# One shape for every product: 256 moving columns, and all moving operands 448 bytes past the stationary blocks modulo 512

## The chip, the cores and the metric

The kernel runs on one core of one Trainium2 chip. The metric is the device time of one execution in microseconds (us), the median of three runs. The core's engines are TensorE (PE in the rows, with its weight loads on a row of their own, PEld), VectorE (DVE), ScalarE (ACT), GpSimd (POOL) and SyncE (SP), which issues the transfers. A product on TensorE has a stationary operand (128 x 128, put in place by a weight load) and a moving operand, whose columns are streamed through it; the result is added up in PSUM.

## The reference

Two layers work on 256 tokens of 2048 features, all in float32. Each layer is a mixer and a gated feed-forward network, each added to the running state `h`.

```python
def reference(x, ...):
    h = x
    for i in range(DEPTH):              # DEPTH = 2
        j = i // 2
        if i % 2 == 0:
            h = h + conv_pool_mixer(h, ...)    # layer 0
        else:
            h = h + short_conv_mixer(h, ...)   # layer 1
        h = h + swiglu(rms_norm(h, ffn_norm[i]), w_gate[i], w_up[i], w_down[i])
    return rms_norm(h, final_norm)

def swiglu(h, w_gate, w_up, w_down):
    return (jax.nn.silu(h @ w_gate) * (h @ w_up)) @ w_down
```

`conv_pool_mixer` multiplies by `w_in` (2048 x 3072), runs a causal convolution of width 31 and four pooling windows, multiplies by small pooling matrices, and then by `w_out` (2048 x 2048). `short_conv_mixer` multiplies by `w_in` (2048 x 6144), runs a convolution of width 3 and two gates, and multiplies by `w_out`. `D_FF` is 5632.

## The kernel before

Activations are held with features on the 128 partitions and the 256 tokens along the row. All weights together are 5904 blocks of 128 x 128; they stand in one long array in the order in which they are used, and SP fetches them 16 blocks at a time. For float32 accuracy each block is split in two parts: `hi`, a rounded copy made by ACT (L124), and `lo`, the rest, made by DVE or, in part of the first stage, POOL (L131). Eight blocks are split at a time; six such pieces are held. The activations are split in the same way, so that a row of a moving operand holds 256 columns of high parts and then 256 columns of low parts (`xs`, `cat`, `y`, `z`). A block's contribution is hi x high + hi x low + lo x high.

`product` issues these on PE in one of two forms:

- **Wide** (L173, L174): one matmul with `hi` stationary and all 512 moving columns, which puts hi x high in the left half of an accumulator and hi x low in its right half, and one with `lo` and 256 columns, added to the right half. Two weight loads, 768 columns. Both feed-forward networks and layer 1's mixer use it: 5226 blocks. What is done with the result then begins with an addition of the two halves: ACT copies the right half to a tile `cross` (L198 in `summed`, L332 in `project`) and DVE adds it (L200, L333).
- **Narrow** (L176, L177, L178): three matmuls of 256 columns into one sum: `hi` on the high part, `hi` on the low part (with `hi` loaded again) and `lo` on the high part. Three weight loads, 768 columns. Layer 0's mixer uses it (656 blocks), and the very last output chunk (22 blocks, by `narrow_end`).

An accumulator `acc` has a PSUM bank of its own in either form; there are five.

The order of the work is that of the code, changed by a scheduler that places instructions by a time model; PE goes through the blocks in the order of the weight array. `matmul_chunks` takes blocks from `next_block`, which keeps the split four pieces ahead of PE. In layer 0's mixer `tick` hands out the steps of the convolution to DVE, ACT and POOL between the products.

The stages, with the names in the rows: layer 0's mixer (0 to 256 us; moving operand `xs`, then `cat`), the first feed-forward network (`xs` and `y`), layer 1's mixer (`xs` and `z`), the second feed-forward network (`xs` and `y`), the final norm.

Where a moving operand begins is set by a constant for each stage: `XS_M0`, `XS_F0` and so on are bytes from the start of a room that is somewhat larger than the operand (`moving`). Every `hi` and `lo` tile of the built program begins 64 bytes past a multiple of 512 in its partition's row, and a block takes 512 bytes, so each stationary block begins there too. A chunk of a moving operand takes 2048 bytes, 1024 for each half. So each stage has one distance between a moving operand's start and a stationary block's start modulo 512. By the addresses in the built program it is:

| moving operand | form | blocks | bytes past the stationary block, modulo 512 |
|---|---|---|---|
| `xs`, layer 0's mixer | narrow | 512 | 288 |
| `cat`, layer 0's mixer | narrow | 144 | 32 |
| `xs`, the later stages | wide | 3584 | 416 |
| `y` and `z` | wide | 1642 | 160 |
| `y`, last chunk | narrow | 22 | 160 |

Of the kernel before, what the change touches and what calls it, by code (L numbers as in the profile page):

```python
# [11 lines left out]
F32 = mybir.dt.float32  # L12
# [5 lines left out]
P = 128  # L18
# [56 lines left out]
KEEP = 8  # L75


XS_M0 = 32
XS_F0 = 160
XS_M1 = 160  # L80
XS_F1 = 160
Y_F0 = 64
Y_F1 = 64
Z_M1 = 64
CAT = 0

POOL_SPLIT = range(96, 24 * NC + 16 + 7 * NC + 8)

# [6 lines left out]
def block_kernel(ctx: ExitStack, tc: tile.TileContext, xT: bass.AP, xtok: bass.AP, vec: bass.AP, wall: bass.AP, out: bass.AP):  # L95
# [72 lines left out]
                if q:  # L168
                    q.popleft()[1]()

    def product(acc, hi, lo, x, first, last, wide):
        if wide:
            nc.tensor.matmul(acc, hi, x, start=first, stop=False, skip_group_check=True)  # L173
            nc.tensor.matmul(acc[:, T:], lo, x[:, :T], start=False, stop=last, skip_group_check=True)  # L174
        else:
            nc.tensor.matmul(acc[:, :T], hi, x[:, :T], start=first, stop=False)  # L176
            nc.tensor.matmul(acc[:, :T], hi, x[:, T:], start=False, stop=False)  # L177
            nc.tensor.matmul(acc[:, :T], lo, x[:, :T], start=False, stop=last)  # L178

    def matmul_chunks(xs, ks, n=1, wide=False, behind=None):  # L180


        accs = [ps.tile([P, 2 * T], F32, name="acc") for _ in range(n)]
        for i, k in enumerate(ks):
            first, last = i == 0, i == len(ks) - 1
            for acc in accs:
                hi, lo = next_block()
                product(acc, hi, lo, xs[:, k, :], first, last, wide)
                tick()
            if behind is not None:  # L190
                behind(k)
        return accs

    phase = [None]

    def summed(acc, name):
        t = phase[0].tile([P, T], F32, name="cross", bufs=3)
        nc.scalar.copy(t, acc[:, T:])  # L198
        s = (phase[0] if name == "pv" else tmp).tile([P, T], F32, name=name, bufs=2)
        nc.vector.tensor_tensor(out=s, in0=acc[:, :T], in1=t, op=ALU.add)  # L200
        return s

    def split(dst, src, scale=None):

# [10 lines left out]
    def col(name, i):  # L215
        return v[:, VECS[name] + i : VECS[name] + i + 1]
# [5 lines left out]
    def moving(room, at, n):  # L222

        return room[:, at // 4 : at // 4 + n * 2 * T].rearrange("p (c t) -> p c t", c=n)
# [96 lines left out]
            nc.vector.tensor_copy(out=r, in_=st)  # L321
            return r

    def project(src, ks, norm=None, wide=False, narrow_end=False):

        for n in range(NC):
            if narrow_end and n == NC - 1:
                wide = False
            (acc,) = matmul_chunks(src, ks, wide=wide)
            if wide:  # L330
                t = phase[0].tile([P, T], F32, name="cross", bufs=3)
                nc.scalar.copy(t, acc[:, T:])  # L332
                nc.vector.tensor_tensor(out=h[:, n, :], in0=h[:, n, :], in1=t, op=ALU.add)  # L333
            nc.vector.tensor_tensor(out=h[:, n, :], in0=acc[:, :T], in1=h[:, n, :], op=ALU.add)  # L334
            if norm is not None:
                norm.add(n)

    def scaled(acc, r, name, wide=False):
        if not wide:
            s = (phase[0] if name == "pv" else tmp).tile([P, T], F32, name=name, bufs=2)  # L340
            nc.vector.tensor_tensor(out=s, in0=acc[:, :T], in1=r, op=ALU.mult)
            return s
        s = summed(acc, name)
        nc.vector.tensor_tensor(out=s, in0=s, in1=r, op=ALU.mult)
        return s


    norm = Norm("mix_norm_e", XS_M0)
    xs = norm.xs
    nc.sync.dma_start(v[:, :NC], vec[:, :NC])  # L350

# [32 lines left out]
    with tc.tile_pool(name="m0", bufs=1) as m0, tc.tile_pool(name="ps_side", bufs=2, space=PSUM) as ps_side:  # L384
# [1 line left out]
        a_in = m0.tile([P, NA, pad + T], F32, name="a_in")  # L386
        nc.gpsimd.memset(a_in[:, :, :pad], 0.0)
        conv = m0.tile([P, NA, T], F32, name="conv")
        cat = moving(m0.tile([P, NA * 2 * T + 32], F32R, name="cat"), CAT, NA)
        total = m0.tile([P, 2, T], F32, name="total")  # L390

        sides, prods, state = {}, {}, {}
# [104 lines left out]
        def gated(acc_v, acc_g, c):  # L497
            gate = scaled(acc_g, r, "gate")
            nc.scalar.activation(gate, gate, AF.Sigmoid)
            val = acc_v[:, :T]  # L500
            nc.vector.tensor_tensor(out=val, in0=val, in1=r, op=ALU.mult)
            nc.vector.tensor_tensor(out=a_in[:, c, pad:], in0=val, in1=gate, op=ALU.mult)
            if c % 2:
                convolve(c - 1)
# [9 lines left out]
        def pooled(g):  # L514


            w = WINDOWS[g]
            xp = m0.tile([P, 2, pp + T], F32, name="xp", bufs=2)
            nc.gpsimd.memset(xp[:, :, :pp], 0.0)
            less = m0.tile([P, 2, T], F32, name="pm", bufs=2)  # L520
            for j in range(2):
                (acc,) = matmul_chunks(xs, every)
                nc.vector.tensor_tensor(out=xp[:, j, pp:], in0=acc[:, :T], in1=r, op=ALU.mult)
                nc.scalar.activation(less[:, j, :], xp[:, j, pp:], AF.Copy, scale=-float(w))
            cur, step = xp, 1
            while step < w:
                nxt = m0.tile([P, 2, pp + T], F32, name="sw", bufs=2)
                lo = pp - (w - 2 * step)
                nc.gpsimd.tensor_tensor(out=nxt[:, :, lo:], in0=cur[:, :, lo:], in1=cur[:, :, lo - step : pp + T - step], op=ALU.add)
                cur, step = nxt, 2 * step  # L530
            nc.gpsimd.tensor_tensor(out=cur[:, :, pp : pp + w - 1], in0=cur[:, :, pp : pp + w - 1], in1=corr[:, g, :, : w - 1], op=ALU.mult)
            nc.gpsimd.tensor_tensor(out=less, in0=cur[:, :, pp:], in1=less, op=ALU.add)
            dst = cat[:, 2 * g : 2 * g + 2, :]
            nc.scalar.activation(dst[:, :, :T], less, AF.Copy, scale=1.0 / w)
            nc.vector.scalar_tensor_tensor(out=dst[:, :, T:], in0=less, scalar=1.0 / w, in1=dst[:, :, :T], op0=ALU.mult, op1=ALU.subtract)
            relief.append(1)
# [8 lines left out]
        for g in POOL_ORDER:  # L545
            for j in range(2):
                (acc,) = matmul_chunks(cat, range(2 * g, 2 * g + 2))
                split(xs[:, 2 * g + j, :], acc[:, :T], col("pool_scale", 2 * g + j))

        project(xs, POOL_CHUNKS)  # L550
        drain()
        norm = Norm("ffn_norm0", XS_F0)
        project(cat, range(NA), norm)

    def swiglu(norm, following, at):
        with tc.tile_pool(name="ffn", bufs=1) as fp:
            phase[0] = fp
            y = moving(fp.tile([P, NH * 2 * T + 32], F32R, name="y"), at, NH)
            r = None
            for half in range(2):  # L560
                for f in range(NH):
                    (acc_g,) = matmul_chunks(norm.xs, every, wide=True)
                    (acc_u,) = matmul_chunks(norm.xs, every, wide=True)
                    if r is None:
                        r = norm.rstd()
                    gate = scaled(acc_g, r, "gate", True)
                    up = scaled(acc_u, r, "val", True)
# [3 lines left out]
                project(y, range(NH), following if half else None, wide=True, narrow_end=half and following.final)  # L571

    x0.close()


    after = Norm("mix_norm_o", XS_M1)
    swiglu(norm, after, Y_F0)


    norm = Norm("ffn_norm1", XS_F1)  # L580
    with tc.tile_pool(name="m1", bufs=1) as m1:
        phase[0] = m1
        z = moving(m1.tile([P, NC * 2 * T + 32], F32R, name="z"), Z_M1, NC)
        pad = SW - 1
        r = None
        for c in range(NC):
            (acc_c,) = matmul_chunks(after.xs, every, wide=True)
            (acc_v,) = matmul_chunks(after.xs, every, wide=True)
            if r is None:
                r = after.rstd()  # L590
            cg = scaled(acc_c, r, "gate", True)
            vv = scaled(acc_v, r, "val", True)
# [8 lines left out]
            (acc_b,) = matmul_chunks(after.xs, every, wide=True)  # L601
            bg = scaled(acc_b, r, "pv", True)
            nc.vector.tensor_tensor(out=bg, in0=bg, in1=co, op=ALU.mult)
            split(z[:, c, :], bg)
        project(z, every, norm, wide=True)


    last = Norm("final_norm", final=True)
    swiglu(norm, last, Y_F1)
# [93 lines left out]
```

## Time and profile before

| | |
|---|---|
| runs | 2094.73 us median, 2094.72 to 2096.01 us (3 runs) |
| span of the profiled execution, first to last instruction | 2093.2 us |
| granted clock of TensorE over the span | 0.996 |
| weight transfers | 365 of 1024 KB, 4.8 us from issue to landing |
| HBM traffic over the span | 188 GB/s |

The profiled execution has no time of its own beside its span; the median of the runs is 1.5 us above that span, which is what lies before the first and after the last instruction. The page of the profile gives busy time by engine, then the chain of waits that ended last, then groups of instructions. The busy time of a matmul contains its way through the array, and one matmul begins before the one before it has ended; how long PE takes for a matmul is therefore read from one start to the next and not from the duration in the row.

### The profile page before, as it was taken

The page shows a single profiled execution, that of the slowest core. Times are in us where ns is not written, and L with a number is a line of the kernel's source. Part 1 is how long each engine was busy: PE and PEld are TensorE (multiplying, and loading weights), DVE is VectorE, ACT ScalarE, POOL GpSimd, SP SyncE. Part 2 cuts the span into 40 slices and gives each one's busy share as a digit, 9 for nine tenths or more (in the row PEclk, how much of TensorE's full clock was granted, in tenths as well). Part 3 has the DMA queues.
Part 4 walks back from the last instruction along what each step waited for, and adds up shares of the span by engine and source line. Part 5 has one row for each costly group of instructions (what it writes and reads, how often), then busy time and mean ns, then how long its engine had stood idle before and what let it go on. Part 6 is the DMA issues. An engine that isn't in the chain of part 4 may idle for free.

```text
span 2093.2 us, 31608 instructions
## 1 busy us (share of the span) xinstructions
PE 2070.2 (99%) x12584; PEld 1850.5 (88%) x12584; DVE 1383.1 (66%) x1979; ACT 1061.8 (51%) x1571; POOL 200.5 (10%) x180
## 2 busy tenths in 40 slices
PE   8998999999999999999999999999999999999998
PEld 8998988888888888888888888888888888888887
DVE  6998766666556666666777777766666556666654
ACT  7886654444444444455444445554444444444453
POOL 2995200000000000011000001100000000000011
PEclk9999999999999999999999999999999999999999
DMA  8555455555555455555555555455555555555551
GB/s 322 190 199 181 151 190 184 193 189 186 196 184 198 182 195 188 188 195 183 189 191 184 198 182 199 181 186 197 182 195 187 190 193 184 199 183 195 187 191 71
DMA packets 56884, 395.53 MB, mean 189 GB/s; under 512 B 6432, under 2 KB 7200, under 8 KB 9760
## 3 DMA queue, kind: packets, MB, share of 16 engines
q1 hardware_dynamic: 56736, 393.52, 51.9%
q8 instruction: 98, 1.61, 0.3%
q14 instruction: 50, 0.41, 0.1%
HBM read 391.39 MB, written 2.10 MB: 188 GB/s over the span
## 4 chain that ended last, share of the span: by engine, by line
PE 98%; DMA 1%; DVE 1%; ACT 0%; SPq 0%; issue 0%; DVEq 0%; ACTq 0%
PE acc L173 57%; PE acc L174 29%; PE acc L176 4%; PE acc L178 4%; PE acc L177 3%; DMA rows<-in_xtok 0%; DMA h<-in_xT 0%; DVE res L620 0%; ACT hi L124 0%; PE st L252 0%; DVE lo L131 0%; PE st L283 0%; SPq L114 0%; ACT conv L492 0%; PE idle L258 0%
## 5 line engine op out<-in xcount | busy, mean ns | idle before, releaser
L131 DVE TENSOR_TENSOR lo<-w,hi 128x1024 fp32r<-128x1024 f32 (+1 forms) x691 | 846.2, 1225 | 634.3 <-ACT hi L124 630.1
L124 ACT CAST hi<-w 128x1024 fp32r<-128x1024 f32 (+1 forms) x740 | 775.5, 1049 | 963.9 <-PE acc L173 615.9
L173 PE MATMUL acc<-xs,hi 128*128 128x512 f32 x3584 | 1243.2, 392 | 0.0
L174 PE MATMUL acc<-xs,lo 128*128 128x256 f32 x3584 | 1002.3, 280 | 0.0
L173 PEld LDWEIGHTS acc<-xs,hi 128*128 128x128 f32 x3584 | 672.7, 188 | 148.5
L174 PEld LDWEIGHTS acc<-xs,lo 128*128 128x128 f32 x3584 | 672.7, 188 | 0.1
L173 PE MATMUL acc<-y,hi 128*128 128x512 f32 x1386 | 480.4, 392 | 0.0
L174 PE MATMUL acc<-y,lo 128*128 128x256 f32 x1386 | 386.8, 280 | 0.0
L173 PEld LDWEIGHTS acc<-y,hi 128*128 128x128 f32 x1386 | 259.9, 188 | 57.2
L174 PEld LDWEIGHTS acc<-y,lo 128*128 128x128 f32 x1386 | 260.2, 188 | 0.4
L314 POOL TENSOR_TENSOR sumsq<-sumsq,sq 128x256 f32<-128x256 f32 x56 | 59.0, 1053 | 1593.0 <-ACT sq L312 1593.0
L176 PE MATMUL acc<-xs,hi 128*128 128x256 f32 x512 | 142.7, 282 | 5.2 <-ACT hi L124 4.2
L177 PE MATMUL acc<-xs,hi 128*128 128x256 f32 x512 | 142.2, 280 | 0.0
L178 PE MATMUL acc<-xs,lo 128*128 128x256 f32 x512 | 140.2, 282 | 0.1
L131 POOL TENSOR_TENSOR lo<-w,hi 128x1024 fp32r<-128x1024 f32 x49 | 118.5, 2440 | 41.4 <-ACT hi L124 41.3
L176 PEld LDWEIGHTS acc<-xs,hi 128*128 128x128 f32 x512 | 96.9, 190 | 6.1 <-ACT hi L124 4.8
L177 PEld LDWEIGHTS acc<-xs,hi 128*128 128x128 f32 x512 | 96.9, 189 | 0.0
L178 PEld LDWEIGHTS acc<-xs,lo 128*128 128x128 f32 x512 | 95.4, 190 | 0.5 <-DVE lo L131 0.5
L173 PE MATMUL acc<-z,hi 128*128 128x512 f32 x256 | 88.7, 392 | 0.0
L198 ACT COPY cross<-acc 128x256 f32<-128x256 f32 x224 | 81.4, 363 | 0.0
L174 PE MATMUL acc<-z,lo 128*128 128x256 f32 x256 | 71.4, 280 | 0.0
L334 DVE TENSOR_TENSOR h<-acc,h 128x256 f32<-128x256 f32 x112 | 47.2, 423 | 18.3 <-PE acc L178 11.9
(134 smaller groups left out, 1199.3 us busy)
## 6 DMA issues: line engine op xcount, KB each, us to landing
w<-in_wall SPq DMA_DIRECT2D x365, 1024.0 KB, 4.8
w<-in_wall SPq DMA_DIRECT2D x7, 512.0 KB, 7.3
rows<-in_xtok SPq DMA_DIRECT2D x2, 1024.0 KB, 8.1
h<-in_xT SPq DMA_DIRECT2D x7, 256.0 KB, 7.2
out<-res SPq DMA_DIRECT2D x2, 512.0 KB, 2.8
out<-res SPq DMA_DIRECT2D x2, 384.0 KB, 2.8
v<-in_vec SPq DMA_DIRECT2D x1, 260.0 KB, 6.6
h<-in_xT SPq DMA_DIRECT2D x2, 128.0 KB, 2.3
```

The source lines that it names most:

```text
L124: nc.scalar.copy(hi[:, : n * P], w)
L131: engine.tensor_tensor(out=lo[:, : n * P], in0=w, in1=hi[:, : n * P], op=ALU.subtract)
L173: nc.tensor.matmul(acc, hi, x, start=first, stop=False, skip_group_check=True)
L174: nc.tensor.matmul(acc[:, T:], lo, x[:, :T], start=False, stop=last, skip_group_check=True)
L176: nc.tensor.matmul(acc[:, :T], hi, x[:, :T], start=first, stop=False)
L177: nc.tensor.matmul(acc[:, :T], hi, x[:, T:], start=False, stop=False)
L178: nc.tensor.matmul(acc[:, :T], lo, x[:, :T], start=False, stop=last)
L198: nc.scalar.copy(t, acc[:, T:])
L314: nc.gpsimd.tensor_tensor(out=self.sums[0], in0=self.sums[0], in1=sq, op=ALU.add)
L334: nc.vector.tensor_tensor(out=h[:, n, :], in0=acc[:, :T], in1=h[:, n, :], op=ALU.add)
```

## The change

`product` has the narrow form alone. `summed` goes, and with it the ACT copies to `cross` and the DVE additions after the wide products; `project` adds the accumulator to `h` in one step, and `scaled` multiplies it by the norm's factor at once. The accumulator tile is 256 columns instead of 512, still in a bank of its own. The rooms of `cat`, `y` and `z` grow by 384 bytes, and three constants set the starts of the moving operands: by the addresses in the built program every one of them then begins 448 bytes past the stationary blocks modulo 512.

```diff
-XS_M0 = 32
-XS_F0 = 160
-XS_M1 = 160
-XS_F1 = 160
-Y_F0 = 64
-Y_F1 = 64
-Z_M1 = 64
-CAT = 0
+XS_AT = 192
+Y_AT = 352
+CAT_AT = 416
...
-    def product(acc, hi, lo, x, first, last, wide):
-        if wide:
-            nc.tensor.matmul(acc, hi, x, start=first, stop=False, skip_group_check=True)
-            nc.tensor.matmul(acc[:, T:], lo, x[:, :T], start=False, stop=last, skip_group_check=True)
-        else:
-            nc.tensor.matmul(acc[:, :T], hi, x[:, :T], start=first, stop=False)
-            nc.tensor.matmul(acc[:, :T], hi, x[:, T:], start=False, stop=False)
-            nc.tensor.matmul(acc[:, :T], lo, x[:, :T], start=False, stop=last)
+    def product(acc, hi, lo, x, first, last):
+        nc.tensor.matmul(acc, hi, x[:, :T], start=first, stop=False)
+        nc.tensor.matmul(acc, hi, x[:, T:], start=False, stop=False)
+        nc.tensor.matmul(acc, lo, x[:, :T], start=False, stop=last)
...
-        accs = [ps.tile([P, 2 * T], F32, name="acc") for _ in range(n)]
+        accs = [ps.tile([P, T], F32, name="acc") for _ in range(n)]
...
-    def summed(acc, name):
-        t = phase[0].tile([P, T], F32, name="cross", bufs=3)
-        nc.scalar.copy(t, acc[:, T:])
-        s = (phase[0] if name == "pv" else tmp).tile([P, T], F32, name=name, bufs=2)
-        nc.vector.tensor_tensor(out=s, in0=acc[:, :T], in1=t, op=ALU.add)
-        return s
...
-    def project(src, ks, norm=None, wide=False, narrow_end=False):
+    def project(src, ks, norm=None):
 
         for n in range(NC):
-            if narrow_end and n == NC - 1:
-                wide = False
-            (acc,) = matmul_chunks(src, ks, wide=wide)
-            if wide:
-                t = phase[0].tile([P, T], F32, name="cross", bufs=3)
-                nc.scalar.copy(t, acc[:, T:])
-                nc.vector.tensor_tensor(out=h[:, n, :], in0=h[:, n, :], in1=t, op=ALU.add)
-            nc.vector.tensor_tensor(out=h[:, n, :], in0=acc[:, :T], in1=h[:, n, :], op=ALU.add)
+            (acc,) = matmul_chunks(src, ks)
+            nc.vector.tensor_tensor(out=h[:, n, :], in0=acc, in1=h[:, n, :], op=ALU.add)
             if norm is not None:
                 norm.add(n)
 
-    def scaled(acc, r, name, wide=False):
-        if not wide:
-            s = (phase[0] if name == "pv" else tmp).tile([P, T], F32, name=name, bufs=2)
-            nc.vector.tensor_tensor(out=s, in0=acc[:, :T], in1=r, op=ALU.mult)
-            return s
-        s = summed(acc, name)
-        nc.vector.tensor_tensor(out=s, in0=s, in1=r, op=ALU.mult)
+    def scaled(acc, r, name):
+        s = (phase[0] if name == "pv" else tmp).tile([P, T], F32, name=name, bufs=2)
+        nc.vector.tensor_tensor(out=s, in0=acc, in1=r, op=ALU.mult)
         return s
...
-            y = moving(fp.tile([P, NH * 2 * T + 32], F32R, name="y"), at, NH)
+            y = moving(fp.tile([P, NH * 2 * T + 128], F32R, name="y"), at, NH)
...
-                    (acc_g,) = matmul_chunks(norm.xs, every, wide=True)
-                    (acc_u,) = matmul_chunks(norm.xs, every, wide=True)
+                    (acc_g,) = matmul_chunks(norm.xs, every)
+                    (acc_u,) = matmul_chunks(norm.xs, every)
```

In layer 0's mixer the order of instructions is the same on every engine before and after; only addresses differ there. From the first feed-forward network on the rows change. On PE, where layer 0's mixer ends (`cat`) and the first feed-forward network begins (`xs`), these rows stood before:

```order
L176 MATMUL acc<-cat,hi 128x256
L177 MATMUL acc<-cat,hi 128x256
L178 MATMUL acc<-cat,lo 128x256
L173 MATMUL acc<-xs,hi 128x512
L174 MATMUL acc<-xs,lo 128x256
L173 MATMUL acc<-xs,hi 128x512
L174 MATMUL acc<-xs,lo 128x256
```

In the changed program the same place reads:

```order
L167 MATMUL acc<-cat,hi 128x256
L168 MATMUL acc<-cat,hi 128x256
L169 MATMUL acc<-cat,lo 128x256
L167 MATMUL acc<-xs,hi 128x256
L168 MATMUL acc<-xs,hi 128x256
L169 MATMUL acc<-xs,lo 128x256
L167 MATMUL acc<-xs,hi 128x256
```

Each block of the later stages has three matmuls in place of two; the order of the blocks is kept. On DVE, in the same network a little later (`gate` and `val` are the two products of one chunk, `lo` the split of weights, `y` the split of the result), the rows before were:

```order
L200 TENSOR_TENSOR gate<-acc,cross 128x256
L344 TENSOR_TENSOR gate<-gate,rstd 128x256
L131 TENSOR_TENSOR lo<-w,hi 128x1024 x2
L200 TENSOR_TENSOR val<-acc,cross 128x256
L344 TENSOR_TENSOR val<-val,rstd 128x256
L569 TENSOR_TENSOR val<-val,gate 128x256
L131 TENSOR_TENSOR lo<-w,hi 128x1024
L207 TENSOR_TENSOR y<-val,y 128x256
```

and they are now:

```order
L318 TENSOR_TENSOR gate<-acc,rstd 128x256
L126 TENSOR_TENSOR lo<-w,hi 128x1024 x2
L318 TENSOR_TENSOR val<-acc,rstd 128x256
L543 TENSOR_TENSOR val<-val,gate 128x256
L126 TENSOR_TENSOR lo<-w,hi 128x1024
L191 TENSOR_TENSOR y<-val,y 128x256
```

One DVE instruction for each product is gone, and on ACT the copy that it waited for; the weight splits keep their places between the others.

More of the change, by code (lines that the diff above doesn't have):

```diff
@@ L169, in drain, with matmul_chunks @@
                     q.popleft()[1]()
-    def product(acc, hi, lo, x, first, last, wide):
-        if wide:
-            nc.tensor.matmul(acc, hi, x, start=first, stop=False, skip_group_check=True)
-            nc.tensor.matmul(acc[:, T:], lo, x[:, :T], start=False, stop=last, skip_group_check=True)
-        else:
[L176 to L180, printed above, removed]
-        accs = [ps.tile([P, 2 * T], F32, name="acc") for _ in range(n)]
+    def product(acc, hi, lo, x, first, last):
+        nc.tensor.matmul(acc, hi, x[:, :T], start=first, stop=False)
+        nc.tensor.matmul(acc, hi, x[:, T:], start=False, stop=False)
+        nc.tensor.matmul(acc, lo, x[:, :T], start=False, stop=last)
+    def matmul_chunks(xs, ks, n=1, behind=None):
+        accs = [ps.tile([P, T], F32, name="acc") for _ in range(n)]
         for i, k in enumerate(ks):
@@ L187, in matmul_chunks @@
                 hi, lo = next_block()
-                product(acc, hi, lo, xs[:, k, :], first, last, wide)
+                product(acc, hi, lo, xs[:, k, :], first, last)
                 tick()
@@ L322, in rstd @@
             return r
-    def project(src, ks, norm=None, wide=False, narrow_end=False):
+    def project(src, ks, norm=None):
         for n in range(NC):
-            if narrow_end and n == NC - 1:
-                wide = False
-            (acc,) = matmul_chunks(src, ks, wide=wide)
-            if wide:
-                t = phase[0].tile([P, T], F32, name="cross", bufs=3)
-                nc.scalar.copy(t, acc[:, T:])
-                nc.vector.tensor_tensor(out=h[:, n, :], in0=h[:, n, :], in1=t, op=ALU.add)
-            nc.vector.tensor_tensor(out=h[:, n, :], in0=acc[:, :T], in1=h[:, n, :], op=ALU.add)
+            (acc,) = matmul_chunks(src, ks)
+            nc.vector.tensor_tensor(out=h[:, n, :], in0=acc, in1=h[:, n, :], op=ALU.add)
             if norm is not None:
                 norm.add(n)
-    def scaled(acc, r, name, wide=False):
-        if not wide:
-            s = (phase[0] if name == "pv" else tmp).tile([P, T], F32, name=name, bufs=2)
-            nc.vector.tensor_tensor(out=s, in0=acc[:, :T], in1=r, op=ALU.mult)
-            return s
-        s = summed(acc, name)
-        nc.vector.tensor_tensor(out=s, in0=s, in1=r, op=ALU.mult)
+    def scaled(acc, r, name):
+        s = (phase[0] if name == "pv" else tmp).tile([P, T], F32, name=name, bufs=2)
+        nc.vector.tensor_tensor(out=s, in0=acc, in1=r, op=ALU.mult)
         return s
-    norm = Norm("mix_norm_e", XS_M0)
+    norm = Norm("mix_norm_e", XS_AT)
     xs = norm.xs
@@ L388, in block_kernel @@
         conv = m0.tile([P, NA, T], F32, name="conv")
-        cat = moving(m0.tile([P, NA * 2 * T + 32], F32R, name="cat"), CAT, NA)
+        cat = moving(m0.tile([P, NA * 2 * T + 128], F32R, name="cat"), CAT_AT, NA)
         total = m0.tile([P, 2, T], F32, name="total")
@@ L499, in gated @@
             nc.scalar.activation(gate, gate, AF.Sigmoid)
-            val = acc_v[:, :T]
+            val = acc_v
             nc.vector.tensor_tensor(out=val, in0=val, in1=r, op=ALU.mult)
@@ L522, in pooled @@
                 (acc,) = matmul_chunks(xs, every)
-                nc.vector.tensor_tensor(out=xp[:, j, pp:], in0=acc[:, :T], in1=r, op=ALU.mult)
+                nc.vector.tensor_tensor(out=xp[:, j, pp:], in0=acc, in1=r, op=ALU.mult)
                 nc.scalar.activation(less[:, j, :], xp[:, j, pp:], AF.Copy, scale=-float(w))
@@ L547, in block_kernel @@
                 (acc,) = matmul_chunks(cat, range(2 * g, 2 * g + 2))
-                split(xs[:, 2 * g + j, :], acc[:, :T], col("pool_scale", 2 * g + j))
+                split(xs[:, 2 * g + j, :], acc, col("pool_scale", 2 * g + j))
         project(xs, POOL_CHUNKS)
         drain()
-        norm = Norm("ffn_norm0", XS_F0)
+        norm = Norm("ffn_norm0", XS_AT)
         project(cat, range(NA), norm)
@@ L561, in swiglu @@
                 for f in range(NH):
-                    (acc_g,) = matmul_chunks(norm.xs, every, wide=True)
-                    (acc_u,) = matmul_chunks(norm.xs, every, wide=True)
+                    (acc_g,) = matmul_chunks(norm.xs, every)
+                    (acc_u,) = matmul_chunks(norm.xs, every)
                     if r is None:
                         r = norm.rstd()
-                    gate = scaled(acc_g, r, "gate", True)
-                    up = scaled(acc_u, r, "val", True)
+                    gate = scaled(acc_g, r, "gate")
+                    up = scaled(acc_u, r, "val")
                     nc.scalar.activation(gate, gate, AF.Silu)
@@ L570, in swiglu @@
                     split(y[:, f, :], up)
-                project(y, range(NH), following if half else None, wide=True, narrow_end=half and following.final)
+                project(y, range(NH), following if half else None)
     x0.close()
-    after = Norm("mix_norm_o", XS_M1)
-    swiglu(norm, after, Y_F0)
-    norm = Norm("ffn_norm1", XS_F1)
+    after = Norm("mix_norm_o", XS_AT)
+    swiglu(norm, after, Y_AT)
+    norm = Norm("ffn_norm1", XS_AT)
     with tc.tile_pool(name="m1", bufs=1) as m1:
         phase[0] = m1
-        z = moving(m1.tile([P, NC * 2 * T + 32], F32R, name="z"), Z_M1, NC)
+        z = moving(m1.tile([P, NC * 2 * T + 128], F32R, name="z"), Y_AT, NC)
         pad = SW - 1
@@ L586, in block_kernel @@
         for c in range(NC):
-            (acc_c,) = matmul_chunks(after.xs, every, wide=True)
-            (acc_v,) = matmul_chunks(after.xs, every, wide=True)
+            (acc_c,) = matmul_chunks(after.xs, every)
+            (acc_v,) = matmul_chunks(after.xs, every)
             if r is None:
                 r = after.rstd()
-            cg = scaled(acc_c, r, "gate", True)
-            vv = scaled(acc_v, r, "val", True)
+            cg = scaled(acc_c, r, "gate")
+            vv = scaled(acc_v, r, "val")
             cv = m1.tile([P, pad + T], F32, name="cv", bufs=2)
@@ L600, in block_kernel @@
                 nc.vector.scalar_tensor_tensor(out=co, in0=cv[:, k : k + T], scalar=v[:, wc + k : wc + k + 1], in1=co, op0=ALU.mult, op1=ALU.add)
-            (acc_b,) = matmul_chunks(after.xs, every, wide=True)
-            bg = scaled(acc_b, r, "pv", True)
+            (acc_b,) = matmul_chunks(after.xs, every)
+            bg = scaled(acc_b, r, "pv")
             nc.vector.tensor_tensor(out=bg, in0=bg, in1=co, op=ALU.mult)
             split(z[:, c, :], bg)
-        project(z, every, norm, wide=True)
+        project(z, every, norm)
     last = Norm("final_norm", final=True)
-    swiglu(norm, last, Y_F1)
+    swiglu(norm, last, Y_AT)
     halves = rsqrt_of(*last.sums, scale=1.0 / D, halves=True)
```

## The prediction

> **What bounds the kernel now.** First the page's busy time, its chain of waits by engine, and then PE's own waits.
>
> ```profile
> PE 2070.2 (99%) x12584; PEld 1850.5 (88%) x12584; DVE 1383.1 (66%) x1979; ACT 1061.8 (51%) x1571; POOL 200.5 (10%) x180
> ...
> PE 98%; DMA 1%; DVE 1%; ACT 0%; SPq 0%; issue 0%; DVEq 0%; ACTq 0%
> ```
>
> ```profile
> PE acc L176 <- ACT hi L124: 4.2, 3, 2.4
> PE acc L176 <- ACT cat L494: 3.4, 1, 3.4
> PE st L283 <- DVE diag L275: 2.8, 1, 2.8
> ```
>
> The chain is PE for 98% of the span, and these are PE's three largest waits for compute engines (us in total, times, longest). All of them are small, and none ends before a wide matmul (L173, L174). So the time is the number of blocks times PE's pace per block, plus layer 0's start and stalls. The pace of the wide form comes from the rows of its line (count, duration, first and last start) and from the order of time:
>
> ```profile
> L173 PE MATMUL acc<-xs,hi x3584: 391/392/478, 256.5 to 1957.5; 128*128 128x512 f32 x200
> ...
> L173 PE MATMUL acc<-z,hi x256: 391/392/400, 1257.6 to 1346.0; 128*128 128x512 f32 x128
> ```
>
> ```profile
> 299.80 0.39 PE L173 MATMUL acc<-xs,hi 128*128 128x512 f32 x1
> 300.03 0.28 PE L174 MATMUL acc<-xs,lo 128*128 128x256 f32 x1
> 300.15 0.39 PE L173 MATMUL acc<-xs,hi 128*128 128x512 f32 x1
> ```
>
> From 1257.6 to 1346.0 stand 256 wide blocks: 88.4 / 255 = **0.3467 us a block**. The second answer splits it: 0.23 for the 512 columns, 0.12 for the 256. The wide operand lies 160 bytes past the blocks there (`z`), 416 past at 300 us (`xs`), and the pace is the same.
>
> The narrow form's pace comes from the windows of layer 0's mixer. The columns are length, then busy time and instructions of PE, PEld, DVE, ACT and POOL, the granted clock, the transfers' share and GB/s:
>
> ```profile
> 60.00:130.00 70.00, 70.00 (x602) 70.00 (x602) 64.51 (x123) 57.68 (x105) 65.57 (x37) 1.00 0.53 196
> 220.00:250.00 30.00, 30.00 (x260) 30.00 (x259) 27.81 (x36) 21.11 (x36) 9.63 (x11) 1.00 0.53 185
> ...
> 210.50:213.00 2.50, 2.50 (x13) 2.50 (x13) 0.70 (x3) 2.50 (x6) 0.00 (x0) 0.50 0.00 0
> ```
>
> ```profile
> L176 PE MATMUL acc<-y,hi x22: 277/280/282, 2072.3 to 2079.7; 128*128 128x256 f32 x22
> ```
>
> Between 60 and 130 us (`xs`, 288 bytes past) 602 matmuls touch the window, two or three of them at its ends: 70 / 600 = 0.1167, so 0.350 a block. Between 220 and 250 us (`cat`, 32 bytes past) it is 30 / 258 = 0.116, the same within the count. At the end (`y`, 160 bytes past) 22 blocks take 7.4 / 21 = 0.3524. Two offsets with one pace and one that is 0.7% slower: an offset does something, but little among these three.
>
> **Where a pass loses time.** The window at 210.5 us ran at half clock (0.50). In order of time:
>
> ```profile
> 211.57 0.41 PE L176 MATMUL acc<-cat,hi 128*128 128x256 f32 x1
> 211.78 0.41 PE L177 MATMUL acc<-cat,hi 128*128 128x256 f32 x1
> 211.99 0.41 PE L178 MATMUL acc<-cat,lo 128*128 128x256 f32 x1
> 212.21 0.41 PE L177 MATMUL acc<-cat,hi 128*128 128x256 f32 x1
> ```
>
> Start to start is 0.213. Half of that, 0.1067, would be 256 columns at full clock with nothing in their way: 0.320 for 768 columns. At full clock a narrow pass takes 0.010 more and a wide block 0.027 more. The other stream, the weight loads, is seen alone where a matmul has one column:
>
> ```profile
> 267.94 0.53 PEld L252 LDWEIGHTS st<-ones,sq 128*128 128x128 f32 x4
> 268.39 0.19 PEld L173 LDWEIGHTS acc<-xs,hi 128*128 128x128 f32 x1
> 268.50 0.19 PEld L174 LDWEIGHTS acc<-xs,lo 128*128 128x128 f32 x1
> ```
>
> Four loads take 0.45 from the first to the load after them, 0.112 each. So a narrow pass can't be shorter than **0.112**, whatever its columns do, and 0.005 of its 0.1167 is neither loads alone nor columns alone. I read that rest as the two streams hindering each other where both read at full speed.
>
> **The change part by part.**
>
> *Wide to narrow, 5226 blocks.* One more load and no more columns. The two bounds for the new pace are 3 x 0.112 = 0.336, if the two streams don't hinder each other at 448 bytes, and 0.3524, the slowest of the three offsets seen; the rows at 288 and 32 give 0.350. Against 0.3467 that is between -0.0107 x 5226 = -55.9 us and +0.0057 x 5226 = +29.8 us, with +17.2 us for 0.350 (+0.0033). No row shows 448. What may decide: in one load 512 bytes of each partition are read, and in one pass of 256 columns 1024, in nearly the same time. The moving address thus gains 512 bytes on the stationary one and, modulo 512, meets it once in each pass: at (512 - 288) / 512 = 44% of the pass, at 94% (32 bytes), at 69% (160), and at 448 bytes at 12%, 14 ns after the start. If the meeting costs the time, it costs nothing where it falls between the end of one load's reading and the start of the next one's, and the trace has a gap for it: 0.1167 a pass against 0.112 a load. Of the offsets named, 448 puts the meeting nearest to that gap. I take 0.336, the row of loads alone: **-55.9 us**. That the offset acts this way is the uncertain step.
>
> *The offset alone, layer 0's mixer and the last chunk.* The 656 blocks up to 256 us are narrow already. At 0.336 for 0.350 PE would need 0.014 x 656 = 9.2 us less. Little of that can arrive: between 60 and 130 us DVE is busy for 64.51 of 70, POOL for 65.57, and a pass that is 4% faster leaves POOL and DVE nothing in hand. In order of time, the chain leaves PE just behind this stretch:
>
> ```profile
> 148.57 1.06 ACT hi L124
> ...
> 152.57 1.78 DVE conv L447 x3
> 154.36 0.61 DVE side L413
> ```
>
> PE waits there for DVE's backlog, and it would wait longer if it came earlier. I take 4 of the 9.2, with 0 and 9.2 as ends. The last chunk gives 22 x (0.3524 - 0.336) = 0.4.
>
> *The additions of the two halves.* ACT's copies and DVE's additions go:
>
> ```profile
> L198 ACT COPY cross<-acc 128x256 f32<-128x256 f32 x224 | 81.4, 363 | 0.0
> ...
> L333 DVE TENSOR_TENSOR h<-h,cross 128x256 f32<-128x256 f32 x79 | 33.2, 420 | 9.8 <-ACT cross L332 9.8
> ...
> L332 ACT COPY cross<-acc 128x256 f32<-128x256 f32 x79 | 29.0, 367 | 25.5 <-PE acc L174 25.5
> ```
>
> ACT loses 81.4 + 29.0 = 110 us of work; DVE loses 33.2 here and as many additions on L200 as L198 has copies, 224 of about 0.42, in all 127 us. PE hides both: it waits for neither in the wide stages, where an accumulator is only wanted again four products later. Cost and gain: nothing. A faster PE stays covered too: eight blocks at 0.336 take 2.7 us, and a split of eight blocks costs
>
> ```profile
> L131 DVE TENSOR_TENSOR lo<-w,hi 128x1024 fp32r<-128x1024 f32 (+1 forms) x691 | 846.2, 1225 | 634.3 <-ACT hi L124 630.1
> L124 ACT CAST hi<-w 128x1024 fp32r<-128x1024 f32 (+1 forms) x740 | 775.5, 1049 | 963.9 <-PE acc L173 615.9
> ```
>
> 1.2 us of DVE and 1.0 us of ACT. The transfers would go from 189 to some 195 GB/s; the first slice of the page shows 322.
>
> *The sum.* -55.9 - 4 - 0.4 = -60.3. The span of 2093.2 becomes 2032.9; the median of the runs stands 1.5 above the span, so **2034 us**.
>
> **The rivals.**
>
> *The offset does nothing (0.24).* Narrow stays at 0.350 to 0.3524, since three of three offsets gave that and the wide form was the same at 160 and 416. The third load then costs more than the half-width products save: 2094.7 + 17.2 = **2112**, and up to 2125 at 0.3524. This is the slower side: it holds from 0.3467 a block, 0.1156 a pass, upward. For it speaks that 288 and 32 agree; against it, that 160 differs from them with nothing else changed, and that at half clock the loss is gone, so it is no fixed cost of a pass. The Trainium skill ("SBUF — State Buffer", Who interferes with whom) gives TensorE two independent read ports and says it never waits on anyone, which would make the offset idle; the 0.3524 beside 0.350 speaks a little against that.
>
> *448 is a bad offset (0.08).* If the meeting early in a pass delays the load and the columns behind it, a pass may reach 0.120 (the 0.12 by which the last two starts of the wide answer stand apart): 0.360 a block, +69.5 and +6.6 in layer 0's mixer, **2171**.
>
> *Half the gain (0.06).* At 0.1153 to 0.1158 a pass the new form equals the wide one: **2090 to 2099**.
>
> *Loads are no bound (0.04).* If a pass could follow its columns alone, 0.320 a block: -0.0267 x 5226 = -139.5, **1951** with layer 0's 4. Against it stand the one-column rows, where loads alone take 0.112. The Trainium skill ("TensorE: Matmul & The Clock Gate", Back-to-back issue gap) gives 262 cycles for 256 columns, by which a block would take an estimated 0.3275 us and the kernel about 1990; the full-clock rows here, 0.1167 a pass, don't agree with it.
>
> **How the numbers follow.** The forecast has 0.58: 0.336 to 0.341 a block, 2034 to 2060. Faster is that and the fourth rival, 0.62; within 0.2% (about what a measurement of this kernel can tell from no change) 0.06; slower 0.24 + 0.08 = 0.32. The range goes from 2020 (0.335 a block, -61.0, and all of layer 0's gain, then 9.8, make 2023; 3 us are left for the rounding of the load's pace) to 2120, which takes in 0.351 a block and so about three quarters of the first rival: 0.56 + 0.06 + 0.18 = 0.80. The forecast's own range is 2020 to 2060.
>
> **What would show it.** In the changed profile the narrow lines' starts in the feed-forward networks: 0.112 apart if the streams no longer hinder each other, 0.1167 if the offset does nothing. Layer 0's mixer is the clean test, since only addresses change there: its rows at 60 to 130 us should show PE no longer full, or more than 602 matmuls in 70 us. `cross` is gone, and no wait of PE should have appeared in the wide stages. The forecast is wrong if that pace stays at or above 0.1156.

## The result and the profile after

| | before | changed |
|---|---|---|
| median of the runs beside each other | 2094.72 us (4 runs, 2094.04 to 2096.01) | 2056.07 us (4 runs, 2054.52 to 2058.93) |
| ratio, with its 95% interval | | 0.9815 [0.9801, 0.9829] |
| span of the profiled execution | 2093.2 us | 2057.1 us (its run: 2058.93) |

The change makes the kernel 1.85% faster. One execution among those reported further down (2085.43 us, of the changed kernel run again) is 1.3% longer than the others of the same kernel and is left out of its ratio. The page of the changed kernel, busy time by engine and then the chain of waits by engine:

```profile
PE 2033.1 (99%) x17810; PEld 2030.1 (99%) x17810; DVE 1276.0 (62%) x1676; ACT 981.6 (48%) x1268; POOL 198.4 (10%) x180
...
PE 98%; DMA 1%; DVE 1%; ACT 0%; SPq 0%; issue 0%; DVEq 0%; ACTq 0%
```

PE is the chain as before. The instructions of DVE and ACT add up to 127 and 109 us less, the work that was named; the busy time falls by 107 and 80 only, because instructions of one engine overlap in the profile. The weight loads now fill the span. The new pace stands in the rows of PE's first matmul of a block (count, duration, first and last start) and in the order of time:

```profile
L167 PE MATMUL acc<-z,hi x256: 276/276/276, 1237.3 to 1324.0; 128*128 128x256 f32 x128
```

```profile
299.72 0.28 PE L167 MATMUL acc<-xs,hi 128*128 128x256 f32 x1
299.83 0.28 PE L168 MATMUL acc<-xs,hi 128*128 128x256 f32 x1
299.94 0.28 PE L169 MATMUL acc<-xs,lo 128*128 128x256 f32 x1
300.06 0.28 PE L167 MATMUL acc<-xs,hi 128*128 128x256 f32 x1
```

From 1237.3 to 1324.0 it is 86.7 / 255 = **0.340 us a block**, 0.1133 a pass; 0.336 had been forecast, 0.3467 stood before. For 5226 blocks that is -0.0067 x 5226 = -35 us; from the first block behind layer 0's mixer to the last block the trace has 34.5 us less. The rest of the 36.1 us between the spans is layer 0's mixer, which ends 1.5 us earlier. Its windows (length, then busy time and instructions of PE, PEld, DVE, ACT, POOL, clock, transfers) show something that the forecast didn't have:

```profile
60.00:130.00 70.00, 70.00 (x596) 70.00 (x596) 64.07 (x122) 56.86 (x104) 64.92 (x37) 1.00 0.54 196
165.00:190.00 25.00, 25.00 (x223) 25.00 (x222) 22.37 (x43) 17.18 (x28) 20.86 (x9) 1.00 0.60 217
220.00:250.00 30.00, 30.00 (x267) 30.00 (x267) 28.59 (x36) 21.09 (x37) 10.37 (x12) 1.00 0.57 203
```

A window counts every matmul that touches it, and one lasts 0.28 us, so the pace of a block is 3 x (window + 0.28) / count. Between 60 and 130 us that gives 0.3537, *slower* than the 0.350 of before; from 165 us on it is 0.340. The offset is 448 bytes in all three.

### The profile page after: what moved, and what is told of

It reads as the page before. It is cut to its first block, busy times and chain, and to the rows that moved or that the text cites. A ratio compares the mean times of both kernels' runs of the same rounds, so it can differ in the third digit from the quotient of the medians.

```text
span 2057.1 us, 40971 instructions
## 1 busy us (share of the span) xinstructions
PE 2033.1 (99%) x17810; PEld 2030.1 (99%) x17810; DVE 1276.0 (62%) x1676; ACT 981.6 (48%) x1268; POOL 198.4 (10%) x180
## 4 chain that ended last, share of the span: by engine, by line
PE 98%; DMA 1%; DVE 1%; ACT 0%; SPq 0%; issue 0%; DVEq 0%; ACTq 0%
PE acc L167 32%; PE acc L168 32%; PE acc L169 32%; DMA rows<-in_xtok 0%; DMA h<-in_xT 0%; DVE res L594 0%; ACT hi L119 0%; PE st L236 0%; PE st L267 0%; SPq L109 0%; ACT conv L466 0%; PE idle L242 0%; DVE conv L421 0%; SPq L327 0%; ACT rows L340 0%
## 5 line engine op out<-in xcount | busy, mean ns | idle before, releaser
L167 PE MATMUL acc<-xs,hi 128*128 128x256 f32 x4096 | 1132.5, 277 | 6.4 <-ACT hi L119 5.3
L168 PE MATMUL acc<-xs,hi 128*128 128x256 f32 x4096 | 1131.7, 277 | 0.0
L169 PE MATMUL acc<-xs,lo 128*128 128x256 f32 x4096 | 1129.7, 277 | 0.1
L167 PEld LDWEIGHTS acc<-xs,hi 128*128 128x128 f32 x4096 | 769.5, 188 | 7.5 <-ACT hi L119 6.2
L168 PEld LDWEIGHTS acc<-xs,hi 128*128 128x128 f32 x4096 | 769.5, 188 | 0.0
L167 PE MATMUL acc<-y,hi 128*128 128x256 f32 x1408 | 388.6, 276 | 0.0
L168 PE MATMUL acc<-y,hi 128*128 128x256 f32 x1408 | 388.6, 276 | 0.0
L167 PEld LDWEIGHTS acc<-y,hi 128*128 128x128 f32 x1408 | 264.3, 188 | 0.0
L168 PEld LDWEIGHTS acc<-y,hi 128*128 128x128 f32 x1408 | 264.3, 188 | 0.0
L318 DVE TENSOR_TENSOR gate<-acc,rstd 128x256 f32<-128x256 f32 x112 | 47.5, 424 | 48.8 <-PE acc L169 48.6
L318 DVE TENSOR_TENSOR val<-acc,rstd 128x256 f32<-128x256 f32 x104 | 44.1, 424 | 47.5 <-PE acc L169 47.3
L167 PE MATMUL acc<-z,hi 128*128 128x256 f32 x256 | 70.7, 276 | 0.0
L168 PE MATMUL acc<-z,hi 128*128 128x256 f32 x256 | 70.7, 276 | 0.0
```

Source lines behind the costliest of these rows:

```text
L167: nc.tensor.matmul(acc, hi, x[:, :T], start=first, stop=False)
L168: nc.tensor.matmul(acc, hi, x[:, T:], start=False, stop=False)
L169: nc.tensor.matmul(acc, lo, x[:, :T], start=False, stop=last)
L318: nc.vector.tensor_tensor(out=s, in0=acc, in1=r, op=ALU.mult)
```

## The experiments

All kernels are edits of the changed kernel or of the one before. "Offset" is the distance of a moving operand from the stationary blocks, modulo 512.

### The shape alone, and the offset alone

The changed kernel with the old offsets:

```diff
-XS_AT = 192
-Y_AT = 352
-CAT_AT = 416
+XS_M0 = 32
+XS_F0 = XS_M1 = XS_F1 = 160
+Y_F0 = Y_F1 = Z_M1 = 64
+CAT_AT = 0
```

> The changed kernel with the old offsets (xs 288 in layer 0's mixer and 416 later, y and z 160, cat 32): the shape alone. Theory A, the offset makes the gain: the blocks of the later stages stay at 0.350 to 0.3524 us, and the time is 2110 to 2126 us. Theory B, the gain comes from the narrow shape itself (one sum, no copies on ACT, no additions on DVE) and the offset is idle: 0.340 us a block and about 2056 us.

```profile
L172 PE MATMUL acc<-z,hi x256: 277/281/283, 1284.7 to 1375.5; 128*128 128x256 f32 x128
```

2143.67 us, ratio 1.0230 [1.0213, 1.0247]. `z` at 160 takes 90.8 / 255 = 0.356 a block, and `xs` at 416 the same 0.356. So theory B falls: the narrow shape by itself costs 49 us. It is slower than theory A's price too, because the 0.3524 that I had taken from the last 22 blocks is not what a long stretch at 160 runs at.

The kernel before with all offsets at 448, wide form kept:

```diff
-XS_M0 = 32
-XS_F0 = XS_M1 = XS_F1 = 160
-Y_F0 = Y_F1 = Z_M1 = 64
-CAT = 0
+XS_M0 = XS_F0 = XS_M1 = XS_F1 = 192
+Y_F0 = Y_F1 = Z_M1 = 352
+CAT = 416
```

> The kernel before with every moving operand 448 bytes past the stationary blocks: the offset alone, wide form kept. Theory A, the two streams hinder each other less at 448 whatever the shape: a wide block falls below 0.3467 us, to 0.326 to 0.335, and the time to 1980 to 2035 us. Theory C, only a pass of 256 columns that is as long as a load has anything to gain at 448: a wide block stays at 0.345 to 0.360, 2085 to 2165 us.

```profile
L173 PE MATMUL acc<-z,hi x256: 388/397/398, 1271.1 to 1361.2; 128*128 128x512 f32 x128
```

2125.84 us, ratio 1.0145 [1.0130, 1.0160]; 90.1 / 255 = 0.3533 a block. Theory C holds: 448 is bad for the wide form. Each half of the change alone makes the kernel slower, by 49 and by 31 us; together they make it 39 us faster. The two are one edit.

### Which offsets, and how exactly

Two scans with another offset in each later stage (only constants differ, as above, and in the second the size of one room). Their times, 2122.06 and 2152.02 us in one run each, mix several offsets, so the paces are read from the stages:

> The changed kernel with another offset in each later stage: xs 480, then 0, then 320; y 384, then 192; z 64; layer 0's mixer stays at 448. Theory A (the place in the pass at which the two addresses meet decides): 480 near 0.340 us a block, 384 between, 0, 64, 192 and 320 at 0.348 or more. Theory D (only the offset modulo 128 matters, so that 64, 192 and 320 are like 448): these three at 0.340, and 0, 384 and 480 elsewhere.

> As the scan before with xs 96, then 224, then 352; y 128, then 256; z 464; layer 0's mixer at 448. Theory A: z at 464 at 0.340 us a block or below, all others at 0.348 or more. Theory D: 96, 224 and 352 alike, 128 and 256 alike, and 464 (80 modulo 128) unlike 448. Both theories leave it open whether any offset reaches 0.335, three loads alone.

Windows of the first scan, in the order 480, 384, 0, 64, 320, 192:

```profile
260.00:480.00 220.00, 220.00 (x1860) 219.95 (x1860) 127.78 (x166) 96.77 (x120) 0.00 (x0) 1.00 0.51 185
510.00:620.00 110.00, 110.00 (x929) 110.00 (x928) 52.76 (x53) 40.02 (x39) 0.00 (x0) 1.00 0.52 189
1010.00:1270.00 260.00, 260.00 (x2168) 259.95 (x2168) 167.35 (x235) 101.24 (x108) 1.40 (x14) 1.00 0.50 182
1280.00:1365.00 85.00, 85.00 (x724) 85.00 (x723) 55.54 (x61) 42.09 (x61) 13.09 (x13) 1.00 0.51 186
1380.00:1600.00 220.00, 220.00 (x1869) 219.95 (x1868) 127.92 (x166) 96.00 (x120) 0.00 (x0) 1.00 0.52 185
1625.00:1735.00 110.00, 110.00 (x973) 110.00 (x972) 54.88 (x56) 42.84 (x41) 0.00 (x0) 1.00 0.54 194
```

Windows of the second scan, in the order 96, 128, 224, 464, 352, 256:

```profile
260.00:480.00 220.00, 220.00 (x1835) 219.94 (x1834) 125.64 (x162) 94.95 (x118) 0.00 (x0) 1.00 0.50 182
510.00:620.00 110.00, 110.00 (x929) 110.00 (x928) 52.28 (x54) 40.85 (x39) 0.00 (x0) 1.00 0.51 183
1020.00:1270.00 250.00, 250.00 (x2114) 249.95 (x2113) 163.00 (x231) 99.40 (x105) 1.39 (x14) 1.00 0.52 186
1288.00:1370.00 82.00, 82.00 (x705) 82.00 (x704) 53.89 (x59) 40.52 (x58) 12.92 (x13) 1.00 0.52 189
1380.00:1600.00 220.00, 220.00 (x1834) 219.94 (x1834) 124.85 (x162) 93.87 (x116) 0.00 (x0) 1.00 0.50 182
1640.00:1740.00 100.00, 100.00 (x835) 100.00 (x835) 47.35 (x47) 35.89 (x36) 0.00 (x0) 1.00 0.52 187
```

The last row of the first scan: 3 x 110.28 / 973 = 0.340 at 192; its first, at 480, 0.3553; at 0 it is 0.360. Theory A falls with this: 480 is next to 448 and bad, 192 is half a period away and good. Theory D falls as well: 64 and 320 (0.3535) are not like 192 and 448. What the runs so far have in common is a period of 256 bytes: every pair that is 256 apart and was run agrees (0 and 256, 64 and 320, 96 and 352, 128 and 384, 160 and 416, 192 and 448, 224 and 480).

Closer to 448:

> The changed kernel with offsets close to 448 (192 modulo 256): layer 0's mixer at 192, xs 440, then 432, then 460; y 456, then 452; z 444. The two scans gave 0.340 us a block at 192 and 448 and 0.350 at 464. Theory A (a meeting of the two addresses that is hidden in a gap): a best offset between the 32-byte steps, 0.335 to 0.338 at one of 440 to 456. Theory E (the streams proceed in steps of some 8 to 16 bytes, and a pass locks to a whole number of them): 0.340 again over a stretch of 8 to 16 bytes, and none below 0.340.

Windows in the order 440, 456, 432, 444, 460, 452:

```profile
260.00:480.00 220.00, 220.00 (x1834) 219.95 (x1834) 125.52 (x162) 94.95 (x117) 0.00 (x0) 1.00 0.50 182
510.00:620.00 110.00, 110.00 (x919) 110.00 (x918) 52.25 (x54) 39.85 (x38) 0.00 (x0) 1.00 0.50 182
1020.00:1270.00 250.00, 250.00 (x2098) 249.95 (x2096) 160.65 (x225) 98.48 (x103) 1.40 (x14) 1.00 0.51 184
1292.00:1380.00 88.00, 88.00 (x744) 88.00 (x744) 57.28 (x62) 43.43 (x62) 13.92 (x14) 1.00 0.51 181
1390.00:1600.00 210.00, 210.00 (x1784) 209.95 (x1783) 121.86 (x158) 91.49 (x114) 0.00 (x0) 1.00 0.52 186
1640.00:1750.00 110.00, 110.00 (x907) 110.00 (x906) 50.90 (x53) 39.86 (x38) 0.00 (x0) 1.00 0.52 182
```

Neither theory: 440 and 456 run at 0.360, 444 at 0.356, and 452, one float32 element beyond 448, at 3 x 110.28 / 907 = 0.365, the slowest of all. 448 isn't the bottom of a valley but a single place among its neighbours 4 bytes away.

The wide form, scanned from 416 to other offsets:

> The kernel before with another offset in each wide stage: xs 416, then 192, then 32; y 448, then 0; z 64; layer 0's mixer at 448 and 192. Theory A' (each form has its own best offset; at 448 the wide form is at 0.3533 us a block however it got there): 416 at 0.3467, y at 448 and xs at 192 at 0.3533 although the stage ahead ran at 0.3467. Theory F (0.3533 at 448 is one of two paces that a stream of passes can be in, carried over from the end of layer 0's mixer, which was at 0.3533 in that run): y at 448 now at 0.3467 or below.

```profile
L173 PE MATMUL acc<-z,hi x256: 392/392/398, 1265.1 to 1354.2; 128*128 128x512 f32 x128
```

`z` at 64 takes 89.1 / 255 = 0.3494. By the starts of successive blocks `xs` at 416 ran at 0.3467, `y` at 448 behind it at 0.3533, `xs` at 192 at 0.3533, `xs` at 32 and `y` at 0 at 0.3467. A' holds: the pace goes with the offset and isn't carried over from the stage ahead.

The offsets that were left:

> Offsets that no run had yet: the wide form in the first feed-forward network, xs 352 and y 128; the narrow form after it, xs 272 (16 modulo 256), z 48, xs 336 (80 modulo 256), y 112; layer 0's mixer at 448. Theory J (448 and 192 are alone: the wide form's best is 0.3467 us a block, the narrow one's 0.340): no stage below these. Theory K (there are other good places among the multiples of 16): a stage below 0.340, down to 0.335.

The narrow stages, in the order 272, 48, 336, 112:

```profile
1000.00:1260.00 260.00, 260.00 (x2194) 259.95 (x2194) 169.01 (x239) 103.76 (x110) 1.52 (x16) 1.00 0.51 184
1275.00:1360.00 85.00, 85.00 (x721) 85.00 (x720) 55.40 (x60) 42.29 (x60) 13.82 (x14) 1.00 0.52 186
1370.00:1600.00 230.00, 230.00 (x1944) 229.95 (x1943) 133.10 (x171) 99.08 (x123) 0.00 (x0) 1.00 0.51 184
1620.00:1730.00 110.00, 110.00 (x973) 110.00 (x972) 54.42 (x56) 43.29 (x41) 0.00 (x0) 1.00 0.55 195
```

112 is a second good place: 973 matmuls in 110 us, 0.340. The wide form got 0.350 at 352 and 0.351 at 128. Theory K had named a stage below 0.340 as its sign, and none came; but 448 and 192 aren't alone, so of theory J only the level holds. Together (us a block in the long stretches, by the starts of successive blocks; offsets modulo 256):

| offset | 0 | 16 | 32 | 48 | 64 | 80 | 96 | 112 | 128 | 160 | 176 | 192 | 208 | 224 |
|---|---|---|---|---|---|---|---|---|---|---|---|---|---|---|
| narrow | 0.360 | 0.356 | 0.350 | 0.355 | 0.353 | 0.355, 0.360 | 0.360 | **0.340** | 0.356 | 0.356 | 0.358 | **0.340** | 0.350 | 0.355 |
| wide | 0.347 | | 0.347 | | 0.349 | | 0.350 | | 0.351 | 0.347 | | 0.353 | | |

An offset alone doesn't fix the pace. At 336 (80 in the table) most of the network's first half ran at 0.355 and its second half at 0.360. At 272 (16) the first two lines here lie between two stalls, the last two behind the second one:

```profile
1011.80 0.28 PE L178 MATMUL acc<-xs,lo 128*128 128x256 f32 x1
...
1012.82 0.28 PE L178 MATMUL acc<-xs,lo 128*128 128x256 f32 x1
...
1017.76 0.28 PE L178 MATMUL acc<-xs,lo 128*128 128x256 f32 x1
...
1018.83 0.28 PE L178 MATMUL acc<-xs,lo 128*128 128x256 f32 x1
```

Three blocks take 1.02 us between the stalls and 1.07 us behind them, 0.340 a block against about 0.356. So the table has the pace in which a long stretch ran, and no run shows that an offset can't do better than its entry.

### The difference or the address

```diff
-    xs_room = act.tile([P, NC * 2 * T + 64], F32R, name="xs")
+    xs_room = act.tile([P, NC * 2 * T + 88], F32R, name="xs")
...
-XS_AT = 192
+XS_AT = 288
```

> The changed kernel with the weights and all that lies behind them 96 bytes further on, and xs too, so that every difference stays 448 and every absolute address modulo 256 changes. Theory A (the difference decides): 0.340 us a block in all later stages, 2052 to 2060 us. Theory I (the address of one of the two streams decides): another pace, 0.350 to 0.360, 2110 to 2160 us.

2056.67 us in its one run, and 0.340 in every later stage (`z` from 1235.2 to 1321.9 us, 86.7 / 255). All addresses of both operands moved by 96 bytes modulo 256 and the pace stayed, so theory A holds for this one shift: the difference decides.

### Fewer moving columns

```diff
-        nc.tensor.matmul(acc, hi, x[:, :T], start=first, stop=False)
-        nc.tensor.matmul(acc, hi, x[:, T:], start=False, stop=False)
-        nc.tensor.matmul(acc, lo, x[:, :T], start=False, stop=last)
+        n = T if first else cols[0]
+        nc.tensor.matmul(acc[:, :n], hi, x[:, :n], start=first, stop=False)
+        nc.tensor.matmul(acc[:, :n], hi, x[:, T : T + n], start=False, stop=False)
+        nc.tensor.matmul(acc[:, :n], lo, x[:, :n], start=False, stop=last)
```

> The changed kernel with fewer moving columns in all but the first block of each product of the feed-forward networks; the rest of the columns' sum is left out. First network: 128 columns, xs at 448 and y at 160. Second: 224 columns in xs and 192 in y, both at 448. Theory G (0.340 is what three loads of this type take, and 448 has no loss left): 0.340 us a block in all four, whatever the columns and the offset. Theory H (loads alone take 0.112 a pass as in the one-column rows, and 0.0013 a pass is still lost at 448): 0.335 with 128 columns at both offsets, 0.335 to 0.340 with 192 and 224.

The stages in order: 128 columns at 448, 128 at 160, all 256 at 448 (layer 1's mixer, for comparison), 224 at 448, 192 at 448. Each product of 16 or 22 blocks has all its columns in the first one. The kernel leaves out part of the sum; its one run took 2043.46 us.

```profile
260.00:490.00 230.00, 230.00 (x2053) 229.95 (x2052) 139.81 (x179) 105.59 (x131) 0.00 (x0) 1.00 0.55 197
500.00:610.00 110.00, 110.00 (x985) 110.00 (x985) 55.51 (x56) 42.84 (x42) 0.00 (x0) 1.00 0.54 195
970.00:1220.00 250.00, 250.00 (x2204) 249.95 (x2203) 168.87 (x237) 103.62 (x109) 1.40 (x14) 1.00 0.54 193
1320.00:1550.00 230.00, 230.00 (x2052) 229.95 (x2052) 139.38 (x179) 104.39 (x129) 0.00 (x0) 1.00 0.54 195
1560.00:1670.00 110.00, 110.00 (x985) 110.00 (x984) 55.38 (x57) 42.97 (x41) 0.00 (x0) 1.00 0.55 199
```

That is 0.3365, 0.3359, 0.3407, 0.3367 and 0.3359, full blocks included. Theory H holds: loads alone take about 0.112 a pass, 0.335 a block, and with half the columns 160 is as good as 448. With 256 columns at 448 some 0.0015 a pass is still there that is not the loads.

### The copies and additions put back

```diff
+            t = phase[0].tile([P, T], F32, name="cross", bufs=3)
+            nc.scalar.activation(t, acc, AF.Copy, scale=0.0)
+            nc.vector.tensor_tensor(out=s, in0=acc, in1=t, op=ALU.add)
+            nc.vector.tensor_tensor(out=s, in0=s, in1=r, op=ALU.mult)
...
+                t = phase[0].tile([P, T], F32, name="cross", bufs=3)
+                nc.scalar.activation(t, acc, AF.Copy, scale=0.0)
+                nc.vector.tensor_tensor(out=h[:, n, :], in0=h[:, n, :], in1=t, op=ALU.add)
```

> The changed kernel with an ACT copy and a DVE addition put back behind every product of the later stages (the copy is scaled by zero, so the sum is the same). Theory A (PE hides this work): the time of the changed kernel, 2052 to 2060 us, and 0.340 us a block. Theory B (part of the gain comes from the work that ACT and DVE lost): slower by 5 us or more, with waits of PE on DVE or ACT in the later stages.

```profile
L324 ACT ACTIVATE cross<-acc 128x256 f32<-128x256 f32 x224 | 84.5, 377 | 0.0
...
L314 ACT ACTIVATE cross<-acc 128x256 f32<-128x256 f32 x80 | 30.4, 379 | 34.4 <-PE acc L169 34.4
```

With 304 copies and as many additions back the ratio is 0.9824 [0.9809, 0.9839], beside 0.9815 [0.9801, 0.9829] without them, and 0.340 a block in every later stage. From the first block behind layer 0's mixer to the last block it is 1789.0 us in this profile and 1788.9 in that of the changed kernel. The 3.3 us by which the spans differ lie ahead of these blocks and behind them; a copy of 0.39 us and an addition of 0.44 for the very last product, which the kernel before doesn't have, stand in the chain there. Theory A holds: that work was hidden.

### The two paces in layer 0's mixer

> The changed kernel unchanged, for the spread of its runs (2054.5 to 2058.9 us). Theory L (after a stall in layer 0's mixer the stream falls into one of two paces, 0.340 or 0.3533 us a block, and keeps it up to the next stall): runs near 2054.5 have 0.340 between 42 and 145 us and runs near 2059 have 0.3533, the profiled run's span says which, and the difference for some 310 blocks is 0.0133 x 310 = 4.1 us. Rival M (the spread comes from the transfers or from the start): the profiled run's span and its pace between 42 and 145 us don't go together.

The same window of the first profile of the changed kernel (run of 2058.93 us) and of this one (run of 2054.51 us), each from its own profile:

```profile
50.00:140.00 90.00, 90.00 (x766) 90.00 (x766) 82.25 (x152) 71.74 (x130) 84.92 (x49) 1.00 0.54 193
```

```profile
50.00:140.00 90.00, 90.00 (x796) 90.00 (x795) 86.25 (x160) 74.75 (x134) 86.77 (x49) 1.00 0.55 198
```

0.3536 against 0.3403 a block in one and the same program, and the spans are 4.5 us apart, 2057.1 and 2052.6. The ratio was 0.9825 [0.9812, 0.9839]. In all eleven profiles with `xs` at 448 or 192 the passes between 50 and 140 us run at one of these two paces, six times at the slow one, and the pace changes only where PE has stood still. That speaks for theory L. The paces of the executions without a profile aren't known.

If the second pace belonged to 448, the other good place might be free of it:

> The changed kernel with every moving operand 112 bytes past the stationary blocks modulo 256 (xs 368, the others 112 modulo 512): the one other place where a stage ran at 0.340 us a block. Theory K (112 is as good as 448 in every stage): 0.340 from 250 us on, and 2052 to 2061 us. With it, theory N (the second pace after a stall, 0.3533, belongs to 448 and 192 and not to the good pace itself): layer 0's mixer always at 0.340, all runs within 2 us, 2050 to 2055 us. Rival J (112 was good for y only, after xs at 336): 0.350 to 0.360 in the xs stages, 2110 us or more.

```profile
50.00:140.00 90.00, 90.00 (x797) 90.00 (x796) 86.32 (x153) 71.59 (x129) 83.22 (x47) 1.00 0.52 187
300.00:480.00 180.00, 180.00 (x1590) 180.00 (x1589) 108.15 (x134) 80.63 (x100) 0.00 (x0) 1.00 0.54 194
```

Theory K holds, 0.340 in every later stage at 368 as at 112. Layer 0's mixer ran at 0.340 throughout in this profile, but the times didn't improve: ratio 0.9821 [0.9808, 0.9835], runs from 2055.27 to 2059.99 us. Theory N fits the pace of this one profile and falls as to the time. The chain of this kernel shows where the time went (start, length, what):

```profile
143.61 0.50 DVE side L390
144.13 0.70 DVE side L392
144.84 0.33 DVE acc L480
145.17 0.40 DVE side L390
145.59 0.50 DVE side L390
146.11 0.71 DVE side L392
```

The chain has left PE for DVE's convolution steps, and PE starts its next product after the stall at 154.6 us, where the profile above has 151.6: the mixer ends at 254.7 us here, at 250.4 there. Why DVE is behind in this run isn't shown. What the spread of 5 us in the runs of 112 consists of was not settled; the state of the passes alone doesn't explain it. The changed kernel stays as good as any that was run.

## Why the prediction was right in its sign and off in its size

- **What bounds the kernel**: PE's pace per block. Right; of the 36.1 us between the two profiled spans 34.5 lie in the stages behind layer 0's mixer, where the pace times 5226 blocks gives 35.0.
- **Wide to narrow at 0.336 a block, -55.9 us**: the mis-sized term. It measured 0.340, -35.0 us, and that is 21 of the 22 us by which the forecast was too low. Loads alone do take 0.335, as the one-column rows had said and the runs with fewer columns confirmed; but 256 columns beside a load still lose some 0.0015 a pass at the best offset.
- **The reason given for 448** (one meeting of the two addresses in each pass, nearest to the gap between two loads) failed. At 480 or 456 the meeting lies as near, and these run at 0.355 and 0.360; 192, where it lies at 62% of the pass, runs at 0.340. That the offset acts at all, and through the difference of the two addresses, was right. The reason read the offset modulo 512; the runs show a period of 256. Why just 112 and 192 modulo 256 are good is open: no run shows it. So that 448 came out well was luck, as far as this reason goes: of the 14 offsets in the table only these two bring the narrow form below the 0.3467 of the kernel before.
- **The rival that the offset does nothing** fell: at the old offsets the same shape takes 2143.7 us. Its price of 2112 to 2125 was too low, since the pace at 160 was read from 22 blocks (0.3524) and is 0.356 over a stage. The Trainium skill's rule that stood with it ("SBUF — State Buffer", Who interferes with whom: TensorE never waits on anyone), read as an idle offset, doesn't hold here: from 0.340 to 0.365 us a block with nothing changed but a difference of addresses. Where the two streams meet no run shows.
- **Loads are no bound** fell too. No stage went below 0.335, with however few columns. The Trainium skill's 262 cycles for 256 columns ("TensorE: Matmul & The Clock Gate", Back-to-back issue gap), an estimated 0.109 us, were reached in none. The Trainium skill gives them there for a matmul by itself, and says that in a stream of pairs the load and the matmul together set the spacing.
- **Layer 0's mixer, 4 of 9.2 us**: 1.5 and 6.0 us in the two profiles of the changed kernel. The cover named, DVE's backlog, showed itself at 112; the second pace, which costs about as much, was not foreseen. It also spoiled what the prediction called the clean test, more than 602 matmuls or an idle PE between 60 and 130 us: the first profile of the changed kernel has 596 there and a full PE, slower than before, although the pace of all later stages had fallen.
- **The additions at nothing**: right, shown by putting them back: the later stages take 1789.0 us with them and 1788.9 without.

## What to carry to other kernels

Where PE's passes and their weight loads are about equally long (0.117 and 0.112 us in the kernel before), look at the addresses: the distance between the moving and the stationary operand can be worth 7% of the pace (0.340 to 0.365 us here), and a few bytes decide. The best distance belongs to a shape of matmul, so that shape and distance have to be tried together; here each alone made the kernel slower. A pace is best read over a whole stage, since a stall can leave a stretch in another one, and an offset is scanned cheaply by giving each stage of one run another one.

## What the runs showed of the hardware that was not expected

- The pace of narrow passes has a period of 256 bytes in the difference of the two operands' addresses, and it isn't smooth: 0.356 us a block at 444, 0.340 at 448, 0.365 at 452.
- At an unchanged offset there can be two steady paces, 0.340 and 0.3533 at 448, 0.340 and 0.356 at 272. At 448 which one a stretch has was decided where PE took up work after a stall, and in the runs here it then held to the next one.
